# Norm sums on VectorE with a second ones-matmul, the input's first rows loaded ahead of the weights, and moved gates, low parts and scans in a two-layer hybrid block

## The chip, the cores and the metric

The kernel runs on one core of a Trainium2 chip. The metric is the time of one execution in device microseconds. Its engines are called here as in the profile: PE (TensorE: matmuls; PEld is its weight load), DVE (VectorE), ACT (ScalarE), POOL (GpSimd) and SP, whose queue issues nearly all DMA transfers. Each engine works through its own list of instructions in a fixed order, and an instruction that waits holds up all those behind it on that engine.

## The reference

Two layers work on a sequence of 1024 tokens with 1024 features. Layer 0 has a mixer of chunked retention and a gated delta rule (GDN), layer 1 a mixer with a gated linear recurrence (RG-LRU); each is followed by a feed-forward block with a short convolution. A root-mean-square norm over the features stands ahead of each of these four parts and at the end.

```python
def _rms(x):
    xf = x.astype(jnp.float32)
    return xf * lax.rsqrt(jnp.mean(xf * xf, axis=-1, keepdims=True) + EPS)

def retention_deltanet_mixer(hn, pos, w_in, conv_w, a_log, dt_bias, out_gain, w_out):
    q_r, k_r, v_r, g_r, q_d, k_d, v_d, g_d, b_d, a_d = jnp.split(hn @ w_in, split_at, axis=-1)
    ...
    beta = jax.nn.sigmoid(b_d.astype(f32))
    g = -jnp.exp(a_log.astype(f32)) * jax.nn.softplus(a_d.astype(f32) + dt_bias.astype(f32))
    y_d = gated_delta_chunkwise(q_d, k_d, v_d, g, beta)
    ...
def conv_ffn(hn, w_up, conv_w, conv_b, w_down):
    up = causal_dwconv(hn @ w_up, conv_w) + conv_b
    gate, val = jnp.split(up, 2, axis=-1)
    return (jax.nn.silu(gate) * val) @ w_down
```

Inside `gated_delta_chunkwise` each chunk of 64 tokens needs a triangular system solved before its values and state can be worked out.

## The kernel before

**Matmuls in three parts.** Features lie on the 128 partitions, tokens along the free axis. A product of two float32 matrices is formed from three matmuls in a reduced float32 format (`fp32r`), 128x128 times 128x512: high by high, low by high, and high by low (L296, L297, L298). 9000 of them make up nearly all of PE's work. The weights come in quarters of 256 KB: SP loads one into a `raw` buffer (L248), ACT rounds it to `whi` (L258), and `wlo`, the rest, is formed by a subtraction (L259), on POOL in the first mixer and on DVE after it (`lo_engine`). In the last part, the down-projection of the second feed-forward block, the tokens are worked in pieces of 512, 256 and 256, and each piece loads and splits its 16 quarters again.

**Order.** The program is written with generators: `project_n` emits matmuls, and after each group it lets "lanes" advance by one step. A lane holds the GDN work (key convolutions, gates, the per-chunk stages, the solution of the triangular system `subst`, its `merge`, the scans). A wait in a lane, `yield from range(k)`, puts off what follows by k groups. The framework then places the instructions on each engine's list by its own estimates; after that all order is fixed.

**The start.** SP loads `cols` (513 columns of per-feature constants, 256 KB), then three weight quarters, then the input `xT` in 16 pieces (8 feature blocks k for each half n of the tokens), with three more weight quarters ahead of k=4. ACT and DVE turn each piece into a high part (L371) and a low part (L372), and 24 matmuls on zeros (L1389) run while nothing else can.

**A norm.** For each k ACT squares the piece (L380 for k=0, into the accumulator; L389 for the others, into one of two buffers), and L391 adds the square to the accumulator. The add is on POOL, or on DVE past a block number called `on_vector`; where there are two accumulators, L394 adds them. Four matmuls with a column of ones (L404 in `norm_tok`) sum over the partitions, DVE (L408) and POOL (L409) form the power -1/2, and L416 in `norm_row` spreads the result over the partitions, in PSUM. There are eight norms of 512 tokens ahead of the four parts, and three in the last part (512, 256 and 256 tokens).

**The operands after a mixer.** `pair_operands` forms the first feed-forward operands from the mixer's output: it copies the spread row from PSUM to SBUF (L543, ACT), multiplies by it (L534, L551), and splits into high (L547, ACT) and low parts (L548, DVE).

**The GDN gates.** `gates()` makes 32 matmuls into two PSUM tiles, evacuates them on DVE (L1054), and transposes the result (L1058). In the program it stands behind the three key convolutions' `conv_tail` (L1098, L1101 on DVE, of 1024 columns each). After `subst`, whose steps are chains of small DVE operations (L1164, L1166), the solution is written to DRAM (L1169, L1171) and read back in another layout (L1185) for `merge` (L1198 on PE).

Of the kernel before, what the change touches and what calls it, by code (L numbers as in the profile page):

```python
# [13 lines left out]
F32 = mybir.dt.float32  # L14
F32R = mybir.dt.float32r
AF = mybir.ActivationFunctionType
ALU = mybir.AluOpType
# [86 lines left out]
class Block:  # L104
    def __init__(self, ctx, tc, I, out, stop=None):
        self.ctx, self.tc, self.nc, self.I, self.out = ctx, tc, tc.nc, I, out
        nc = tc.nc
        pool = lambda n, b, **k: ctx.enter_context(tc.tile_pool(name=n, bufs=b, **k))
        self.perm = pool("perm", 1)
        self.wraw_p = pool("wraw", 7)  # L110
        self.kept = pool("kept", 4)
        self.parts = pool("parts", 1)
        self.wsp = pool("wsp", RING)
        self.tp = pool("tp", 3)
        self.sm = pool("sm", 2)
# [61 lines left out]
    def quarter_order(self):  # L177
# [8 lines left out]
        for layer in range(2):  # L186
# [11 lines left out]
            o += [x for _ in range(2 + layer) for x in out(f"ffn_d{layer}", 1)]  # L198
# [56 lines left out]
    def split_quarter(self, raw, eng, w=HALF):  # L255
# [4 lines left out]
        return hi, lo  # L260

# [103 lines left out]
    def norm_step(self, st, k, gain, n):  # L365
# [7 lines left out]
        self.square_step(st, k, src)  # L373

    def square_step(self, st, k, src, w=HALF, on_vector=KT):

        nc = self.nc
        if k in (0, on_vector):
            acc = (st["bufs"][0 if k == 0 else 3] if "bufs" in st else self.t())[:, 0:w]
            nc.scalar.activation(acc, src, AF.Square)  # L380
            st.setdefault("acc", []).append(acc)
            return
# [7 lines left out]
        eng = nc.vector if k > on_vector else nc.gpsimd  # L390
        eng.tensor_tensor(st["acc"][-1], st["acc"][-1], sq, ALU.add)  # L391
        if on_vector < k == KT - 2:
            a, b = st["acc"]
            nc.vector.tensor_tensor(b, a, b, ALU.add)  # L394
            st["acc"] = [b]
# [48 lines left out]
    def part(self, ys, name, groups, sl, each):  # L444
# [27 lines left out]
    def down_x(self, ys, name, gain):  # L472

        def then(n, st, m, h):
            self.norm_step(st, m, gain, n)
# [4 lines left out]
    def down_pairs(self, ys, name, gain):  # L480
# [3 lines left out]
        def then(n, st, m, h):  # L484
            st["bufs"] = [self.halo[n][:, 4 + HALF:]] + [b[:, 4:4 + HALF] for b in self.halo] + \
                [self.R[:, n * HALF:(n + 1) * HALF]]
            self.square_step(st, m, h, on_vector=5)
# [34 lines left out]
    def pair_operands(self, st, n, gain, gap):  # L522
# [19 lines left out]
        row = (self.R[:, 0:HALF], self.halo[1][:, 4 + HALF:4 + T])[n]  # L542
        A.copy(row, st["row"])  # L543
# [255 lines left out]
    def final(self, ys, name):  # L799
# [13 lines left out]
        def part(t0, w, left):  # L813
# [4 lines left out]
            def each(m, h):  # L818
                self.square_step(st, m, h, w, on_vector=4 if t0 > 0 else KT)
                for f in left.get(m, ()):  # L820
                    f()
            self.part(ys, name, self.groups(1), sl, each)
            return st, sl

        run = self.run
# [17 lines left out]
    def rglru(self, gain):  # L843
        nc, I = self.nc, self.I
        V, A = nc.vector, nc.scalar

        sm = lambda name: self.perm.tile([P, 8], F32, name=name)
# [12 lines left out]
        xr, st = {}, {}  # L860
        stack = ExitStack()
        pool = stack.enter_context(self.tc.tile_pool(name="lru", bufs=1))
# [112 lines left out]
    def mix0(self, gain):  # L975
# [8 lines left out]
        self.og = self.perm.tile([P, 1], F32, name="og")  # L984
        self.nc.vector.tensor_scalar(self.og, self.col("out_gain", 0), 0.5, None, ALU.mult)
# [16 lines left out]
    def _mix0(self, room):  # L1002
# [385 lines left out]
        for _ in range(24):  # L1388
# [17 lines left out]
        for n in range(2):  # L1406
            sl = slice(n * HALF, (n + 1) * HALF)
            st = {}
# [11 lines left out]
        for h in range(3):  # L1420
            conv_tail("k", h, bufs[h], H[h])
        gdn += [gates()]
        self.step(self.lanes["gdn"])
        for h in range(3):
            gdn += [a_stage(h, i) for i in range(2)]
        conv_head("k", 3, K[3])
        gdn += [a_stage(3, i) for i in range(2)]

        def subst():
# [7 lines left out]
            yield from range(8)  # L1437
# [29 lines left out]
        self.lo_engine = V  # L1467
        gdn = self.lane("gdn", 2, 0)
        gdn += [scan(n) for n in range(NCH)]
# [14 lines left out]
    def _mix0_out(self, gain, gd):  # L1484
        nc, I = self.nc, self.I
        V = nc.vector

# [106 lines left out]
```

## Time and profile before

| | |
|---|---|
| median of 3 runs | 2300.38 us (2290.4 to 2300.4) |
| the profiled execution | 2299.97 us |
| its span, first to last instruction | 2298.2 us |
| mean granted TensorE clock | 0.985 |
| busy: DVE, ACT, POOL | 1714.5, 1094.5, 209.0 us |
| DMA | 307.45 MB, 133 GB/s over the span |

The profile gives busy times by engine, the span in 40 slices, and groups of instructions by source line with their number, mean duration and the idle time ahead of them. "Waits" lists the time that an engine stood still by the instruction that then came and the one that released it. "Windows" gives the same busy times for chosen stretches, with the granted clock of PE. The "timeline" has single instructions with their start and duration. A line of the profile names a source line of the kernel before; the changed kernel's lines stand up to about 20 further on.

### The profile page before, as it was taken

The page shows a single profiled execution, that of the slowest core. Times are in us where ns is not written, and L with a number is a line of the kernel's source. Part 1 is how long each engine was busy: PE and PEld are TensorE (multiplying, and loading weights), DVE is VectorE, ACT ScalarE, POOL GpSimd, SP SyncE. Part 2 cuts the span into 40 slices and gives each one's busy share as a digit, 9 for nine tenths or more (in the row PEclk, how much of TensorE's full clock was granted, in tenths as well). Part 3 has the DMA queues.
Part 4 walks back from the last instruction along what each step waited for, and adds up shares of the span by engine and source line. Part 5 has one row for each costly group of instructions (what it writes and reads, how often), then busy time and mean ns, then how long its engine had stood idle before and what let it go on. Part 6 is the DMA issues. An engine that isn't in the chain of part 4 may idle for free.

```text
span 2298.2 us, 30084 instructions
## 1 busy us (share of the span) xinstructions
PE 2248.9 (98%) x10784; PEld 1823.5 (79%) x10784; DVE 1714.5 (75%) x2532; ACT 1094.5 (48%) x1748; POOL 209.0 (9%) x160
## 2 busy tenths in 40 slices
PE   8999999999999999999999999999999999999997
PEld 7777788887888888888778888888788888877787
DVE  6886666556888888887874577768888888878747
ACT  5332433224655555554432466665555555553333
POOL 5331111220200000000000200002000000000003
PEclk9998999999999999999999999999999999999999
DMA  4242422414224544536465311142245444375554
GB/s 152 71 126 80 125 77 84 133 60 158 85 82 157 173 157 154 176 111 221 162 199 180 93 55 65 62 152 74 69 161 179 152 169 170 110 240 169 165 186 156
DMA packets 201110, 307.45 MB, mean 134 GB/s; under 512 B 31584, under 2 KB 89088, under 8 KB 200960
## 3 DMA queue, kind: packets, MB, share of 16 engines
q1 hardware_dynamic: 200528, 303.95, 40.2%
q8 instruction: 85, 1.39, 0.3%
q10 hardware_dynamic: 432, 1.58, 0.2%
q14 instruction: 65, 0.53, 0.1%
HBM read 214.73 MB, written 90.72 MB: 133 GB/s over the span
## 4 chain that ended last, share of the span: by engine, by line
PE 85%; DMA 6%; DVE 6%; issue 1%; ACT 1%; SPq 0%; POOL 0%; POOLq 0%; DVEq 0%; ACTq 0%
PE ps L296 26%; PE ps L298 26%; PE ps L297 26%; DMA s<-pf_dram 1%; DMA raw<-in_ffn_w_dram 1%; DVE t L1098 1%; DMA t<-yf_dram 1%; DVE l L1164 1%; DMA h<-in_xT_dram 1%; DMA t<-sf_dram 0%; DVE s L548 0%; PE pc L416 0%; DVE l L1166 0%; PE pc L1305 0%; PE pc L298 0%
## 5 line engine op out<-in xcount | busy, mean ns | idle before, releaser
L296 PE MATMUL ps<-s,whi 128*128 128x512 f32 (+1 forms) x3000 | 1188.5, 397 | 11.3 <-ACT whi L258 4.2
L297 PE MATMUL ps<-s,whi 128*128 128x512 f32 (+1 forms) x3000 | 1167.2, 389 | 10.7 <-DVE s L548 5.2
L298 PE MATMUL ps<-s,wlo 128*128 128x512 f32 (+1 forms) x3000 | 1164.6, 389 | 1.4 <-DVE wlo L259 1.4
L258 ACT CAST whi<-raw 128x512 fp32r<-128x512 f32 (+1 forms) x662 | 398.0, 605 | 740.0 <-PE ps L297 652.2
L296 PEld LDWEIGHTS ps<-s,whi 128*128 128x128 f32 x3000 | 568.3, 189 | 138.4 <-ACT whi L258 8.5
L297 PEld LDWEIGHTS ps<-s,whi 128*128 128x128 f32 x3000 | 569.2, 190 | 135.8 <-DVE s L548 6.7
L298 PEld LDWEIGHTS ps<-s,wlo 128*128 128x128 f32 x3000 | 568.1, 189 | 132.8 <-DVE wlo L259 2.1
L259 DVE TENSOR_TENSOR wlo<-raw,whi 128x512 fp32r<-128x512 f32 x632 | 428.7, 683 | 96.1 <-ACT whi L258 90.5
L670 DVE SCALAR_TENSOR_TENSOR t<-halo,cols,t 128x1024 f32<-128x1024 f32 x176 | 221.6, 1281 | 2.4 <-ACT t L668 1.2
L643 DVE TENSOR_TENSOR halo<-ps,kept 128x512 f32<-128x512 f32 (+1 forms) x138 | 92.0, 668 | 108.0 <-PE ps L298 107.7
L391 POOL TENSOR_TENSOR t<-t 128x512 f32<-128x512 f32 (+1 forms) x41 | 54.0, 1317 | 1295.2 <-ACT t L389 684.3
L653 DVE TENSOR_TENSOR h<-ps,h 128x512 f32<-128x512 f32 x112 | 77.0, 689 | 79.0 <-PE ps L298 78.8
L668 ACT ACTIVATE t<-halo,cols 128x1024 f32<-128x1024 f32 x88 | 109.4, 1246 | 15.7 <-DVE halo L643 9.0
L638 ACT COPY kept<-ps 128x512 f32<-128x512 f32 (+1 forms) x138 | 77.0, 558 | 1.4 <-PE ps L298 1.4
L461 DVE TENSOR_TENSOR h<-ps,h 128x512 f32<-128x512 f32 (+1 forms) x72 | 45.2, 627 | 28.9 <-PE ps L298 28.9
L259 POOL TENSOR_TENSOR wlo<-raw,whi 128x512 fp32r<-128x512 f32 x30 | 44.7, 1496 | 140.0 <-ACT whi L258 109.0
L755 DVE TENSOR_TENSOR t<-t 128x1024 f32<-128x1024 f32 x44 | 53.7, 1220 | 0.0
L738 ACT CAST s<-t 128x512 fp32r<-128x512 f32 x64 | 39.6, 622 | 26.3 <-DMA t<-sf_dram 17.2
L361 DVE TENSOR_TENSOR halo<-ps,R 128x512 f32<-128x512 f32 x38 | 25.9, 686 | 34.6 <-PE ps L298 32.9
L750 ACT ACTIVATE t<-t 128x1024 f32<-128x1024 f32 x44 | 46.8, 1063 | 8.0 <-DVE t L670 8.0
L1098 DVE SCALAR_TENSOR_TENSOR t<-halo,cols,t 128x1024 f32<-128x1024 f32 x33 | 46.4, 1414 | 3.8 <-ACT t L1096 3.4
L739 DVE TENSOR_TENSOR s<-t,s 128x512 fp32r<-128x512 f32 x64 | 42.6, 689 | 7.4 <-ACT s L738 7.0
(270 smaller groups left out, 1837.7 us busy)
## 6 DMA issues: line engine op xcount, KB each, us to landing
raw<-in_ffn_up_dram SPq DMA_DIRECT2D x176, 256.0 KB, 2.8
s<-pf_dram SPq DMA_DIRECT2D x96, 256.0 KB, 5.6
yf_dram<-t SPq DMA_DIRECT2D x32, 512.0 KB, 2.9
sf_dram<-t SPq DMA_DIRECT2D x64, 256.0 KB, 3.0
t<-sf_dram SPq DMA_DIRECT2D x64, 256.0 KB, 4.0
raw<-in_ffn_w_dram SPq DMA_DIRECT2D x64, 256.0 KB, 3.2
raw<-in_mix_in_dram SPq DMA_DIRECT2D x62, 256.0 KB, 3.0
pf_dram<-t SPq DMA_DIRECT2D x48, 256.0 KB, 3.0
```

Source lines behind the costliest of these rows:

```text
L258: self.nc.scalar.copy(hi[:, 0:w], raw[:, 0:w])
L259: eng.tensor_tensor(lo[:, 0:w], raw[:, 0:w], f32(hi[:, 0:w]), ALU.subtract)
L296: mm(ps, whi, xhi, start=start, stop=False)
L297: mm(ps, whi, xlo, start=False, stop=False)
L298: mm(ps, wlo, xhi, start=False, stop=stop)
L391: eng.tensor_tensor(st["acc"][-1], st["acc"][-1], sq, ALU.add)
L638: A.copy(kept[o], ps)
L643: V.tensor_tensor(dst(i, j), v(ps), v(kept[k]), ALU.add)
L653: V.tensor_tensor(h(*to[o]), ps.rearrange("p (h c) -> p h c", c=256), h(*to[o]), ALU.add)
L668: A.activation(t, buf[:, 2:2 + T], AF.Identity, scale=w(0), bias=self.col(f"ffn_cb{layer}", tile_i))
L670: V.scalar_tensor_tensor(t, buf[:, 2 + j:2 + j + T], w(j), t, ALU.mult, ALU.add)
L1098: V.scalar_tensor_tensor(c, buf[:, 1 + j:1 + j + T], w(j), c, ALU.mult, ALU.add)
```

## The change

It has eight parts.

1. The first 40 columns of `cols` (the gains) are loaded alone, the other 473 after the first half of the input. Each input piece is loaded ahead of the weights, the zero matmuls go from 24 to 14, and a piece's square is formed after the next piece's high and low part.
2. All squares are added on DVE. The last one (k=7) is not added: `norm_tok` takes it as a second accumulator, so that it makes eight matmuls where it made four (four where it made two for 256 tokens). L391's POOL adds and L394 are gone.
3. `pair_operands` reads the spread row from PSUM; the copy L543 is gone.
4. The first mixer's low parts of the weights are formed on DVE.
5. `gates()` stands ahead of the three key convolutions' tails, the last keys' `a_stage` comes two steps later, `subst` ends with two more empty steps, and the scans start six steps later.
6. In the last part the 16 weight quarters are loaded and split once and kept for all three pieces.
7. `rglru`'s small constants move into that layer's own pool, and `og` into `_mix0_out`; both were formed at the program's start before.
8. Nothing in the code of the retention's queries and gates is altered.

```diff
-        nc.sync.dma_start(self.cols, I["cols"])
+        self.ngain = COLS["gdn_conv"][0]
+        nc.sync.dma_start(self.cols[:, 0:self.ngain], I["cols"][:, 0:self.ngain])
...
-        self.lo_engine = nc.gpsimd
+        self.lo_engine = nc.vector
...
-            o += [x for _ in range(2 + layer) for x in out(f"ffn_d{layer}", 1)]
+            if layer == 0:
+                o += [x for _ in range(2) for x in out("ffn_d0", 1)]
...
+    def load_kept(self, src, i):
+        w = src.shape[1]
+        raw = self.raw()[:, 0:w]
+        self.nc.sync.dma_start(raw, src)
+        place = [self.slots1(j)[:, 0:w] for j in (i, i + 1)]
+        self.split_half(raw, place)
+        return place
...
         nc.scalar.activation(sq, src, AF.Square)
-        eng = nc.vector if k > on_vector else nc.gpsimd
-        eng.tensor_tensor(st["acc"][-1], st["acc"][-1], sq, ALU.add)
-        if on_vector < k == KT - 2:
-            a, b = st["acc"]
-            nc.vector.tensor_tensor(b, a, b, ALU.add)
-            st["acc"] = [b]
+        if k == KT - 1:
+            st["acc"].append(sq)
+        else:
+            nc.vector.tensor_tensor(st["acc"][0], st["acc"][0], sq, ALU.add)
...
-                    hi, lo = self.quarter((name + "ab"[u], m))
+                    if kept is None:
+                        hi, lo = self.quarter((name + "ab"[u], m))
+                    else:
+                        if (u, m) not in kept:
+                            kept[u, m] = self.load_kept(self.I[name + "ab"[u]][m], 4 * m + 2 * u)
+                        hi, lo = kept[u, m]
...
-        row = (self.R[:, 0:HALF], self.halo[1][:, 4 + HALF:4 + T])[n]
-        A.copy(row, st["row"])
+        row = st["row"]
...
-        for _ in range(24):
+        for _ in range(14):
             PE.matmul(ps[:, 0:P], warm[:, 0:P], warm[:, 0:P], start=True, stop=True)
...
             for k in range(KT):
-                if n == 0 and k in (0, 4):
-                    load_w(k // 4)
                 nc.sync.dma_start(H[k][:, sl], I["xT"][k * P:(k + 1) * P, sl])
-                self.norm_step(st, k, "g_mix0", n)
+                src[k] = self.norm_step(st, k, "g_mix0", n)
+                if n == 0 and k in (0, 3):
+                    load_w(k // 3)
+                if k:
+                    self.square_step(st, k - 1, src[k - 1])
+            self.square_step(st, KT - 1, src[KT - 1])
             if n == 0:
+                nc.sync.dma_start(self.cols[:, self.ngain:], I["cols"][:, self.ngain:])
...
-        for h in range(3):
-            conv_tail("k", h, bufs[h], H[h])
         gdn += [gates()]
         self.step(self.lanes["gdn"])
         for h in range(3):
+            conv_tail("k", h, bufs[h], H[h])
+        for h in range(3):
             gdn += [a_stage(h, i) for i in range(2)]
         conv_head("k", 3, K[3])
-        gdn += [a_stage(3, i) for i in range(2)]
+        gdn += [iter(range(2))] + [a_stage(3, i) for i in range(2)]
...
             subst_store(*sub)
-            yield from range(8)
+            yield from range(10)
...
-        gdn += [scan(n) for n in range(NCH)]
+        gdn += [iter(range(6))] + [scan(n) for n in range(NCH)]
```

What this does to the lists of the engines is shown at three places. The first is the head of ACT's list in the kernel before. `s_94` is a high part of the input, `h_86` and `h_87` its first pieces, `whi` a weight's high part, and DMAHW names a transfer that a row waits for.

```order
L1069 ACT_TABLE_LOAD
L1069 ACTIVATE l_114<-cols 128x4 [waits DMAHW0_49]
L1403 CAST whi<-raw 128x512 [waits DMAHW1_49]
L1403 CAST whi<-raw 128x512 [waits DMAHW2_49]
L1403 CAST whi<-R 128x512 [waits DMAHW3_49]
L960 ACTIVATE sple<-sple 128x8 [waits DVE_49]
L371 ACTIVATE s_94<-h_86,cols 128x512 [waits DMAHW4_49]
L380 ACTIVATE t<-h_86 128x512
L371 ACTIVATE s_94<-h_87,cols 128x512 [waits DMAHW5_49]
```

The same place in the changed kernel, where L383 is the old L371, L1417 the old L1403 and L392 the old L380:

```order
L383 ACT_TABLE_LOAD [waits DMAHW1_49]
L383 ACTIVATE s_94<-h_86,cols 128x512 [waits DMAHW0_49]
L1417 CAST whi<-raw 128x512 [waits DMAHW2_49]
L1417 CAST whi<-raw 128x512 [waits DMAHW3_49]
L1417 CAST whi<-R 128x512 [waits DMAHW4_49]
L383 ACTIVATE s_94<-h_87,cols 128x512 [waits DMAHW5_49]
L392 ACTIVATE t<-h_86 128x512
```

The first input piece now stands ahead of the weights, and the table load, which waited for nothing, waits for that piece's transfer.

The second place is DVE's list around the evacuation of the gates' two PSUM tiles (`t<-ps,R` 32x512) in the kernel before. The rows of 128x1024 are the tails of the key convolutions.

```order
L1101 SCALAR_TENSOR_TENSOR h_86<-h_86,t 128x1024 [waits Activation_49]
L1098 SCALAR_TENSOR_TENSOR t<-halo_97,cols,t 128x1024 [waits DVE_49]
L1098 SCALAR_TENSOR_TENSOR t<-l_114,cols,t 128x1024 [waits DVE_49]
L1101 SCALAR_TENSOR_TENSOR h_87<-h_87,t 128x1024 [waits Activation_49]
L1098 SCALAR_TENSOR_TENSOR t<-l_114,cols,t 128x1024 [waits DVE_49]
L1054 TENSOR_TENSOR t<-ps,R 32x512 [waits PE_49] x2
L1101 SCALAR_TENSOR_TENSOR h_88<-h_88,t 128x1024 [waits Activation_49]
```

In the changed kernel L1068 is the old L1054, L1112 the old L1098:

```order
L1068 TENSOR_TENSOR t<-ps,R 32x512 [waits PE_49]
L1112 SCALAR_TENSOR_TENSOR t<-halo_96,cols,t 128x1024 [waits Activation_49,Pool_49]
L1112 SCALAR_TENSOR_TENSOR t<-halo_97,cols,t 128x1024 [waits Activation_49,Pool_49]
L1112 SCALAR_TENSOR_TENSOR t<-halo_96,cols,t 128x1024 [waits DVE_49]
L1068 TENSOR_TENSOR t<-ps,R 32x512 [waits PE_49]
L1112 SCALAR_TENSOR_TENSOR t<-halo_96,cols,t 128x1024 [waits DVE_49]
```

Both evacuations stand at the head of the tails, with three tail rows between them, instead of behind all but one of the tail rows. On PE's list the first transposes still come after the gates' 32 matmuls, now 12 projection matmuls behind them, before 34.

The third place is the end of `subst` on DVE's list before. The rows on `l_114` are the solution, the copy L1170 its last step, and the rows `<-ps,R` evacuate projections.

```order
L1166 TENSOR_TENSOR l_114<-l_114 128x2x30 [waits DVE_49]
L1164 TENSOR_TENSOR l_114<-l_114 128x31 [waits DVE_49]
L1166 TENSOR_TENSOR l_114<-l_114 128x31 [waits DVE_49]
L1170 COPY l_114<-l_114 128x1024 [waits DVE_49]
L361 TENSOR_TENSOR t<-ps,R 128x512 [waits PE_49]
L999 SCALAR_TENSOR_TENSOR t<-t 128x1024 [waits Activation_49]
```

In the changed kernel L1180 is the old L1166, L1178 the old L1164, L1184 the old L1170:

```order
L1180 TENSOR_TENSOR l_112<-l_112 128x2x30 [waits DVE_49]
L262 TENSOR_TENSOR wlo<-raw,whi 128x512 [waits DMAHW2_49,PE_49,Activation_49]
L1178 TENSOR_TENSOR l_112<-l_112 128x31 [waits DVE_49]
L1180 TENSOR_TENSOR l_112<-l_112 128x31 [waits DVE_49]
L1184 COPY l_112<-l_112 128x1024 [waits DVE_49]
L373 TENSOR_TENSOR halo_96<-ps,R 128x512 [waits PE_49]
L262 TENSOR_TENSOR wlo<-raw,whi 128x512 [waits DMAHW4_49,Activation_49]
```

Low parts of weights (`wlo`) now stand between the steps. The evacuation behind the copy is that of the projection group that ends with PE's 600th projection matmul; before it was that of the 576th or so. The first `merge` matmul stands on PE's list behind 660 projection matmuls, before behind 614.

More of the change, by code (lines that the diff above doesn't have):

```diff
@@ L441, in steps, with part @@
         self.after(slots, go)
-    def part(self, ys, name, groups, sl, each):
+    def part(self, ys, name, groups, sl, each, kept=None):
         w = sl.stop - sl.start
@@ L474, in then @@
         def then(n, st, m, h):
-            self.norm_step(st, m, gain, n)
+            self.square_step(st, m, self.norm_step(st, m, gain, n))
             if m == KT - 1:
@@ L484, in then @@
         def then(n, st, m, h):
-            st["bufs"] = [self.halo[n][:, 4 + HALF:]] + [b[:, 4:4 + HALF] for b in self.halo] + \
-                [self.R[:, n * HALF:(n + 1) * HALF]]
-            self.square_step(st, m, h, on_vector=5)
+            st["bufs"] = [self.halo[n][:, 4 + HALF:]] + [b[:, 4:4 + HALF] for b in self.halo]
+            self.square_step(st, m, h)
             if m == KT - 1:
@@ L818, in each @@
             def each(m, h):
-                self.square_step(st, m, h, w, on_vector=4 if t0 > 0 else KT)
+                self.square_step(st, m, h, w)
                 for f in left.get(m, ()):
                     f()
-            self.part(ys, name, self.groups(1), sl, each)
+            self.part(ys, name, self.groups(1), sl, each, kept)
             return st, sl
+        kept = {}
         run = self.run
@@ L845, in rglru @@
         V, A = nc.vector, nc.scalar
-        sm = lambda name: self.perm.tile([P, 8], F32, name=name)
+        xr, st = {}, {}
+        stack = ExitStack()
+        pool = stack.enter_context(self.tc.tile_pool(name="lru", bufs=1))
+        sm = lambda name: pool.tile([P, 8], F32, name=name)
         sp = sm("sp")
@@ L1486, in _mix0_out @@
         V = nc.vector
+        self.og = self.perm.tile([P, 1], F32, name="og")
+        V.tensor_scalar(self.og, self.col("out_gain", 0), 0.5, None, ALU.mult)
         order = (4, 5, 6, 0, 7, 1, 2, 3)
```

18 lines of the change are left out of this document (6 added, 12 removed).

## The prediction

> **What bounds the kernel.** I read the page first, then PE's waits, then windows around the longest of them.
>
> ```profile
> PE 2248.9 (98%) x10784; PEld 1823.5 (79%) x10784; DVE 1714.5 (75%) x2532; ACT 1094.5 (48%) x1748; POOL 209.0 (9%) x160
> PE 85%; DMA 6%; DVE 6%; issue 1%; ACT 1%; SPq 0%; POOL 0%; POOLq 0%; DVEq 0%; ACTq 0%
> ```
>
> PE is busy 98% and carries 85% of the chain that ended last. The number of large matmuls doesn't change, so time can be won only where PE stands still (2298.2 - 2248.9 = 49 us) or runs slowly. The waits on PE say whom it stood for (engine, tile and line that waited, the releaser; us in total, times, longest):
>
> ```profile
> PE ps L297 <- DVE s L548: 5.2, 6, 1.4
> PE ps L297 <- DVE s L372: 5.1, 2, 4.8
> PE pc L404 <- DVE t L391: 3.2, 1, 3.2
> PE pc L1285 <- DMA l<-v_dram: 3.1, 1, 3.1
> PE ps L296 <- ACT s L547: 3.1, 2, 1.5
> PE pc L1058 <- DVE t L1054: 3.0, 1, 3.0
> PE pc L1198 <- DMA l<-t_dram: 2.5, 1, 2.5
> PE ps L298 <- DVE wlo L259: 1.4, 1, 1.4
> ```
>
> They make 26.6 us, and the change touches each of these places. Behind such a wait the granted clock falls. The windows around them (length; then PE, PEld, DVE, ACT, POOL busy; clock; DMA share; GB/s):
>
> ```profile
> 21.00:32.00 11.00, 8.90 (x25) 7.35 (x26) 9.68 (x22) 5.19 (x9) 4.09 (x4) 0.53 0.30 107
> 74.00:80.00 6.00, 5.73 (x22) 4.41 (x23) 3.84 (x12) 1.80 (x4) 2.43 (x4) 0.72 0.13 44
> 80.00:120.00 40.00, 38.07 (x196) 30.88 (x195) 34.28 (x78) 14.73 (x29) 10.96 (x7) 1.00 0.28 78
> 200.00:226.00 26.00, 23.53 (x180) 15.85 (x180) 8.78 (x17) 8.96 (x18) 2.56 (x2) 0.61 0.20 44
> 284.00:292.00 8.00, 4.91 (x22) 4.05 (x21) 3.94 (x6) 0.00 (x0) 4.16 (x3) 0.79 0.32 95
> 640.00:666.00 26.00, 21.65 (x138) 19.48 (x137) 20.00 (x23) 12.78 (x23) 1.02 (x1) 0.80 0.07 21
> 1612.00:1636.00 24.00, 19.55 (x127) 17.58 (x127) 19.81 (x22) 12.87 (x21) 1.02 (x1) 0.86 0.08 23
> ```
>
> A clock of c over w us means that PE did (1-c)w less than it could: 5.2 us at 21, 1.7 at 74, 10.1 at 200, 1.7 at 284, 5.2 and 3.4 at the two places where `pair_operands` works. So waits and clock together are some 50 us that the change could reach.
>
> **The change part by part**, against the profiled execution (2299.97 us, 0.4 below the median).
>
> *The start.*
>
> ```profile
> 0.73 1.28 ACT L1069 ACT_TABLE_LOAD   x1 [0.73 <-PEq L1586]
> 3.53 0.21 ACT L1069 ACTIVATE l<-cols 128x4 f32<-128x4 f32 x1 [1.51 <-DMA cols<-in_cols_dram]
> 7.72 0.72 ACT L371 ACTIVATE s<-h,cols 128x512 fp32r<-128x512 f32 x1 [0.84 <-DMA h<-in_xT_dram]
> 8.50 0.51 PE L296 MATMUL ps<-s,whi 128*128 128x512 f32 x1
> 15.21 6.61 POOL L391 TENSOR_TENSOR t<-t 128x512 f32<-128x512 f32 x4 [0.43 <-ACT t L389]
> 20.19 0.63 ACT L380 ACTIVATE t<-h 128x512 f32<-128x512 f32 x1 [1.10 <-POOL t L391]
> 23.10 0.79 PE L297 MATMUL ps<-s,whi 128*128 128x512 f32 x1 [4.79 <-DVE s L372]
> ```
>
> The first input piece was the fifth transfer and reached ACT at 7.72. Now only 40 columns stand ahead of it. I take its landing at 3.5, where `cols` landed before (the ACT row at 3.53); the table load now waits for it and adds its 1.28, the high part 0.72 and 0.7 for the weight behind it: first matmul at 6.2, **2.3 us** earlier. The 14 zero matmuls cover most of that time. The stall at 18.3 is ACT waiting for POOL's adds at 1.65 us each (6.61/4), which hold the two square buffers; on DVE an add takes 0.69 (row below). The 4.8 us go; what is late next is the first norm's last square, for which I leave 1.0. Without the stall the clock stretch of 5.2 goes too; I take 4.5. The two norms here have 16 more ones-matmul records:
>
> ```profile
> 594.67 0.39 PE L298 MATMUL ps<-s,wlo 128*128 128x512 f32 x1
> 594.90 0.95 PE L404 MATMUL pc<-ones,R 128*128 128x1 f32 x8
> L391 DVE TENSOR_TENSOR R<-R,halo x8: 684/692/695, 587.5 to 1610.2; 128x512 f32<-128x512 f32 x8
> L543 ACT COPY R<-pc x2: 587/587/587, 599.7 to 1569.7; 128x512 f32<-128x512 f32 x2
> ```
>
> Eight records take 0.95 us, about 0.9 of it on PE's path: -1.8. Sum of the start: 2.3 + 4.8 - 1.0 + 4.5 - 1.8 = **+9** (0 if the transfers hold the start, 11 at best).
>
> *The gates.*
>
> ```profile
> 72.35 1.28 DVE L1098 SCALAR_TENSOR_TENSOR t<-l,cols,t 128x1024 f32<-128x1024 f32 x1
> 73.55 1.27 DVE L1054 TENSOR_TENSOR t<-ps,R 32x512 f32<-32x512 f32 x2
> 74.27 0.43 PE L1058 MATMUL pc<-ident,t 32*128 32x32 f32 x4 [2.99 <-DVE t L1054]
> ```
>
> The evacuations waited behind the tails. Now three tail rows of 1.28 stand between them, 3.8 us, while the second tile's 16 matmuls take 3.7 (16 x 0.23, from a large matmul's start at 594.67 to the next row's at 594.90), and the transposes come 12 matmuls, 2.8 us, later. The wait goes, and with it the clock stretch: 3.0 + 1.7 = **+4.7** (3 to 5).
>
> *Low parts on DVE, in the first mixer.*
>
> ```profile
> L259 POOL TENSOR_TENSOR wlo<-raw,whi 128x512 fp32r<-128x512 f32 x30 | 44.7, 1496 | 140.0 <-ACT whi L258 109.0
> L259 DVE TENSOR_TENSOR wlo<-raw,whi 128x512 fp32r<-128x512 f32 x632 | 428.7, 683 | 96.1 <-ACT whi L258 90.5
> L1098 DVE SCALAR_TENSOR_TENSOR t<-halo,cols,t 128x1024 f32<-128x1024 f32 x33 | 46.4, 1414 | 3.8 <-ACT t L1096 3.4
> ```
>
> DVE gets 30 x 0.683 = 20.5 us. It had 34.28 of 40 us busy from 80 to 120; five or six more low parts would make it 38. Against that, L1098 has a mean of 1414 where one with POOL idle takes 1280 ns: 33 x 0.134 = 4.4 us come back from this line alone. DVE stays just under full, so I take -3 (0 if hidden, -20.5 if none is).
>
> *`subst` and `merge`.*
>
> ```profile
> 195.69 1.13 DVE L1170 COPY l<-l 128x1024 f32<-128x1024 f32 x1
> 202.48 0.31 PE L1198 MATMUL pc<-l,h 32*32 32x32 f32 x2 [2.47 <-DMA l<-t_dram]
> ```
>
> From the copy to `merge` 6.8 us pass (write and read of DRAM). PE's list had 38 matmuls (8.8 us) between the projection group evacuated behind the copy and `merge`; now 60 (14.0), but of the 5.2 us between these some 2 are used up, since the steps of `subst` share DVE with low parts. I count 3 us more slack against 2.5 of wait: the wait goes and the clock stretch behind it, of which I take 8.5 of 10.1: **+11** (0 to 12).
>
> *Scans.*
>
> ```profile
> 278.30 0.43 SPq L1454 DMA_DIRECT2D v_dram<-t  x1
> 285.67 0.32 SPq L1269 DMA_DIRECT2D l<-v_dram  x1
> ```
>
> The first scan matmul, L1285, waits for the last v to be written to DRAM and read back, 7.4 us from one issue to the next and then the landing. This chain stays. But `merge` starts later, so that some 30 more of its records stand on PE's list between the v projections and L1285: 30 x 0.14 (26 us for 180 records at 200) = 4 us of cover against a wait of 3.1. The wait goes, and half of 1.7: **+4** (0 to 5).
>
> *`pair_operands`, twice.* Gone are the copy (0.59) and an add on DVE (0.69); eight more records are added (-0.9, twice per place): 2 x (2 x 1.3 - 1.8) = 1.6, and a little from squares that no longer queue behind POOL, say **+2**; the clock stretches of 5.2 and 3.4 I leave as they are (+7 if they go). *The two norms behind the first feed-forward block:* their chains of squares run beside matmuls, their added records don't: 2 x 0.9 = **-1.8**.
>
> *The last part.*
>
> ```profile
> 2284.76 0.28 PE L298 MATMUL ps<-s,wlo 128*128 128x256 f32 x1
> 2286.34 0.43 DVE L394 TENSOR_TENSOR t<-t 128x256 f32<-128x256 f32 x1
> ```
>
> The last matmul ends at 2285.0, the span 13.2 us later. The add of the two accumulators (L394) and that of the last square behind it leave this tail, 0.9 us, and the evacuation of the last piece, which came to DVE behind such adds, follows PE sooner; I take 13.2 to 10.5. The 1.4 us for a low part (L259 among the waits) go, since none is formed any more in the last two pieces. Costs: 0.9 + 0.45 records. +2.7 + 1.4 - 1.3 = **+3**. The constants moved to `rglru` are small operations beside 98% PE: 0.
>
> Sum: 9 + 4.7 - 3 + 11 + 4 + 2 - 1.8 + 3 = 29; 2300 - 29 = **2271 us**.
>
> **A rule against it.** The wait ahead of `merge` was 2.47 us, and the clock then stood at 0.61 for 26 us. The Trainium skill, "TensorE: Matmul & The Clock Gate" (section "HAM oscillation"), states that PE must not idle for more than about 3.4 us. By that rule the wait at 200 is too short to have cost the clock, something else slows PE there, and the time would be 2282 (the first rival below). The trace speaks against the figure: at 71 a wait of 2.99 us is followed by 0.72 as well, and before L1285 one of 3.1 by 0.79, both under 3.4.
>
> **The rivals.**
>
> *The clock stays low among merges* (0.22). Merges are many small matmuls (180 records in 26 us, against 196 in 40 at full clock), so they may themselves keep the clock low, and the wait may only shift. Then 11 are lost: 2282. For it: the clock stayed low for 20 us after a short wait. Against it: it was full while PE was fed at 80 to 120, with small matmuls among the large.
>
> *DVE becomes the bound of the first mixer* (0.14). If none of the 20.5 us hides, 17.5 more than I took are lost: 2288. For it: 34.28 of 40. Against it: POOL's tensor operations slow DVE, and go.
>
> *The transfers hold the start* (0.08). Seven weights and constants and 16 pieces come over the same queue in any order; if the second half of the input is late anyway, the start's 9 are lost: 2280.
>
> *Doubled ones-matmuls bring the clock down* (0.05): slower. Sixteen records of one column in a row take 1.8 us in which PE does almost nothing; with a short wait beside them they could start a stretch as at 21, 5.2 us. Eleven norms cost up to 57, and from the sixth on (29/5.2) the gain is gone; with eight, 2313. Against it: the block of eight at 594.90 is followed by full speed.
>
> *The change doesn't do all it says.* The moved retention gates show in no line of the diff; that part is worth 0 and is in no sum.
>
> **How the numbers follow.** The forecast has 0.51: 2260 to 2281, its lower end with one pair's clock gained, its upper with the scan and pair terms missing and DVE a little worse. The rivals have 0.49 together and lie from 2280 to 2288, but for the slower one at 2313. A range of 2257 to 2290 leaves out that one, and the upper half of the DVE case. What a measurement can tell from no change is about 0.5%, 11.5 us: faster means below 2289. The forecast, the first and third rival and somewhat over a third of the second lie there, less something for two of them coming together: 0.80. Same is 0.14. Slower is 0.06, the last rival and a hundredth for DVE holding up more than its own work.
>
> **What would show it.** PE's waits without L372 at 4.8, L1058, L1198 and L1285; a clock near 1.0 from 20 to 30 and through the merges; the first large matmul near 6.2; L404's successor with 160 records; no POOL low parts. Wrong: PE waiting for low parts or evacuations between 60 and 220 with DVE full (DVE case), a low clock among merges without a wait ahead (first rival), or new stretches of low clock behind the norms.

## The result, and the profile after

The changed kernel takes 2270.18 us (median of 4, 2267.84 to 2270.97), the kernel before 2297.33 (2290.4 to 2300.4): a ratio of 0.9884, 95% interval 0.9857 to 0.9911. With the comparisons below the kernel before ran 40 times, from 2287.7 to 2301.4 us. Its profiled execution, at 2299.97, was among its long ones; the changed kernel's, at 2267.84, is the fastest of its four, which lie within 3.1 us. So the two traces differ by more than the medians.

Here is the page's line of busy times for the changed kernel, and the rows that head PE's waits now:

```profile
PE 2240.0 (99%) x10844; PEld 1821.3 (80%) x10844; DVE 1702.1 (75%) x2576; ACT 1073.4 (47%) x1712; POOL 78.8 (3%) x73
PE ps L308 <- ACT whi L261: 4.7, 6, 1.3
PE ps L309 <- DVE s L562: 2.3, 2, 1.1
PE ps L308 <- ACT s L561: 2.1, 2, 1.0
PE pc L1389 <- DVE l L1394: 1.8, 2, 0.9
PE pc L414 <- ACT t L401: 0.9, 1, 0.9
```

PE idles for 26 us of its span of 2266.0, where it idled for 49. Of the waits quoted for the kernel before, those at the start (L372, now L384), the gates (L1058, now L1072), `merge` (L1198, now L1212), the first scan (L1285, now L1299) and the low part (L259) are gone. Those at the pairs (L547 and L548, now L561 and L562) are halved: 8.3 us to 4.4. The last norm's wait went from 3.2 to 0.9.

The windows of the changed kernel, with the same columns as before; its merges run from 193 to 250 us:

```profile
21.00:32.00 11.00, 10.82 (x57) 8.84 (x57) 9.74 (x19) 7.31 (x14) 1.51 (x1) 1.00 0.34 119
74.00:80.00 6.00, 6.00 (x27) 4.83 (x26) 5.16 (x15) 3.36 (x4) 0.00 (x0) 1.00 0.25 83
150.00:190.00 40.00, 40.00 (x175) 32.32 (x175) 36.59 (x79) 8.07 (x10) 0.00 (x0) 1.00 0.37 129
205.00:245.00 40.00, 40.00 (x475) 28.15 (x474) 26.07 (x47) 23.24 (x51) 0.00 (x0) 1.00 0.47 115
608.00:634.00 26.00, 22.97 (x161) 21.71 (x160) 20.51 (x23) 12.85 (x21) 1.01 (x1) 0.87 0.05 17
1580.00:1606.00 26.00, 22.89 (x163) 21.70 (x162) 19.77 (x22) 12.87 (x22) 1.01 (x1) 0.87 0.04 11
```

The clock is full everywhere in the first mixer, through 475 PE records in 40 us at the merges too. It still falls at both pair sites. DVE is at 36.59 of 40 us from 150 to 190, and PE doesn't wait there.

To see where the time went, the matmul records of the three lines L296 to L298 (L308 to L310 after; 9096 in each trace) are numbered by their start. The table gives the start of the n-th in both profiled executions:

| n | what lies before it | before | after | gained so far | by this stretch |
|---|---|---|---|---|---|
| 144 | the start | 55.48 | 46.65 | 8.8 | 8.8 |
| 264 | the gates | 96.66 | 83.07 | 13.6 | 4.8 |
| 614 | per-chunk stages, `subst` | 199.61 | 181.84 | 17.8 | 4.2 |
| 1700 | merges and scans | 584.66 | 550.78 | 33.9 | 16.1 |
| 2200 | first pair site | 695.31 | 660.43 | 34.9 | 1.0 |
| 5500 | layer 0's feed-forward with its norms, part of layer 1's mixer | 1475.40 | 1444.01 | 31.4 | -3.5 |
| 6260 | the rest of that mixer, second pair site | 1645.89 | 1614.47 | 31.4 | 0.0 |
| 8600 | second feed-forward | 2198.16 | 2168.80 | 29.4 | -2.0 |
| end | the last part | 2298.18 | 2266.01 | 32.2 | 2.8 |

### The profile page after: what moved, and what is told of

Same layout as the page of the kernel before. It is cut to its first block, busy times and chain, and to the rows that moved or that the text cites. A ratio compares the mean times of both kernels' runs of the same rounds, so it can differ in the third digit from the quotient of the medians.

```text
span 2266.0 us, 29902 instructions
## 1 busy us (share of the span) xinstructions
PE 2240.0 (99%) x10844; PEld 1821.3 (80%) x10844; DVE 1702.1 (75%) x2576; ACT 1073.4 (47%) x1712; POOL 78.8 (3%) x73
## 4 chain that ended last, share of the span: by engine, by line
PE 92%; DVE 3%; DMA 3%; issue 1%; ACT 1%; POOL 0%; SPq 0%; POOLq 0%; DVEq 0%; ACTq 0%
PE ps L308 28%; PE ps L309 28%; PE ps L310 28%; DMA t<-sf_dram 1%; PE pc L414 1%; DMA t<-y_dram 1%; PE pc L426 0%; PE pc L1319 0%; PE pc L309 0%; PE pc L310 0%; PE pc L308 0%; PE pc L1338 0%; PE pc L1361 0%; PE pc L1252 0%; DVE s L562 0%
## 5 line engine op out<-in xcount | busy, mean ns | idle before, releaser
L308 PE MATMUL ps<-s,whi 128*128 128x512 f32 (+1 forms) x2856 | 1132.4, 397 | 9.6 <-ACT whi L261 4.7
L309 PE MATMUL ps<-s,whi 128*128 128x512 f32 (+1 forms) x2856 | 1121.4, 393 | 3.9 <-DVE s L562 2.3
L310 PE MATMUL ps<-s,wlo 128*128 128x512 f32 (+1 forms) x2856 | 1118.4, 392 | 0.0
L261 ACT CAST whi<-raw 128x512 fp32r<-128x512 f32 x614 | 373.1, 612 | 713.3 <-PE ps L309 623.9
L308 PEld LDWEIGHTS ps<-s,whi 128*128 128x128 f32 x2856 | 538.9, 189 | 137.0 <-ACT whi L261 7.9
L309 PEld LDWEIGHTS ps<-s,whi 128*128 128x128 f32 x2856 | 540.0, 189 | 127.7 <-DVE s L753 5.7
L310 PEld LDWEIGHTS ps<-s,wlo 128*128 128x128 f32 x2856 | 538.7, 189 | 124.9 <-DVE wlo L262 0.9
L262 DVE TENSOR_TENSOR wlo<-raw,whi 128x512 fp32r<-128x512 f32 x614 | 410.3, 673 | 76.9 <-ACT whi L261 71.3
L684 DVE SCALAR_TENSOR_TENSOR t<-halo,cols,t 128x1024 f32<-128x1024 f32 x176 | 221.7, 1279 | 2.3 <-ACT t L682 1.1
L419 POOL TENSOR_TENSOR rtok<-rtok,npow 128x4 f32<-128x4 f32 (+1 forms) x11 | 11.4, 1032 | 1782.8 <-DVE rtok L418 1728.8
L401 ACT ACTIVATE t<-h 128x512 f32<-128x512 f32 (+1 forms) x49 | 27.2, 562 | 46.8 <-DVE h L477 40.8
L308 PE MATMUL ps<-s,s 128*128 128x256 f32 (+1 forms) x144 | 46.1, 320 | 0.0
L310 PE MATMUL ps<-s,s 128*128 128x256 f32 (+1 forms) x144 | 45.8, 318 | 0.0
```

What stands on the lines that cost most here:

```text
L261: self.nc.scalar.copy(hi[:, 0:w], raw[:, 0:w])
L262: eng.tensor_tensor(lo[:, 0:w], raw[:, 0:w], f32(hi[:, 0:w]), ALU.subtract)
L308: mm(ps, whi, xhi, start=start, stop=False)
L309: mm(ps, whi, xlo, start=False, stop=False)
L310: mm(ps, wlo, xhi, start=False, stop=stop)
L684: V.scalar_tensor_tensor(t, buf[:, 2 + j:2 + j + T], w(j), t, ALU.mult, ALU.add)
```

## The experiments

Ten kernels ran: changed kernels with one part undone, and kernels before with one part or one number changed. Times are medians; "against the changed kernel" is against 2270.18. The runs of different comparisons may be on different chips, so differences of a microsecond or two are left to the traces.

**The low parts back on POOL.**

```diff
-        self.lo_engine = nc.vector
+        self.lo_engine = nc.gpsimd
...
+        self.lo_engine = V
         gdn = self.lane("gdn", 2, 0)
         gdn += [iter(range(6))] + [scan(n) for n in range(NCH)]
```

> The changed kernel with the first mixer's low parts of the weights back on POOL, all else as changed. On PE's list this also moves the first merge matmul from behind 660 projection matmuls back to behind 621, though subst still ends with ten empty steps. Theory: the later merge came with the low parts, not with the empty steps; so the wait ahead of merge (about 2.5 us) and a clock near 0.6 for some 20 us come back, and waits on DVE among the per-chunk stages too: 2270 becomes 2279 to 2286. Rival: the low parts only load DVE, and merge is covered by the other edits: 3 us faster than the changed kernel, 2267, clock full from 180 to 210.

It took 2287.66 us (2283.52 to 2292.43), 17.5 above the changed kernel; 0.9972 of the kernel before, 0.9959 to 0.9985. That is above what the theory gave, and the rival has the wrong sign. Its PE waits between 60 and 240 us, and the window behind the start of merge:

```profile
PE pc L1088 <- DVE l L1085: 3.7, 1, 3.7
PE pc L1212 <- DMA l<-t_dram: 3.0, 1, 3.0
PE pc L1137 <- DVE h L1149: 1.5, 2, 0.8
198.00:222.00 24.00, 24.00 (x217) 16.45 (x216) 10.55 (x20) 10.40 (x21) 2.34 (x2) 0.64 0.20 41
```

Merge's wait and its low clock are back (0.64 over 24 us), though subst's two extra empty steps are still there. The gates, which are still early, meet a wait one step later in their chain, at L1088. DVE's rows from 48 to 200 us show one reason. The convolution tails and the first line of `subst`, of this kernel and then of the changed one (busy us, mean ns):

```profile
L1112 DVE SCALAR_TENSOR_TENSOR t<-halo,cols,t 128x1024 f32<-128x1024 f32 x21 | 29.8, 1428 | 0.1
L1178 DVE TENSOR_TENSOR l<-l 128x31 f32<-128x31 f32 (+15 forms) x31 | 14.5, 469 | 0.8
```

```profile
L1112 DVE SCALAR_TENSOR_TENSOR t<-halo,cols,t 128x1024 f32<-128x1024 f32 x24 | 30.4, 1276 | 0.7 <-ACT t L1110 0.6
L1178 DVE TENSOR_TENSOR l<-l 128x31 f32<-128x31 f32 (+15 forms) x31 | 10.5, 339 | 1.4 <-DMA l<-l_dram 0.8
```

The same DVE operations take 12% and 38% longer in the mean. A few rows make this difference, as the shortest, median and longest of the 31 rows of `subst` show (ns, the same two kernels):

```profile
L1178 DVE TENSOR_TENSOR l<-l x31: 192/375/1431, 150.3 to 187.8; 128x31 f32<-128x31 f32 x2, 128x60 f32<-128x60 f32 x2, 128x87 f32<-128x87 f32 x2, 128x112 f32<-128x112 f32 x2
L1178 DVE TENSOR_TENSOR l<-l x31: 183/358/426, 143.5 to 182.9; 128x31 f32<-128x31 f32 x2, 128x60 f32<-128x60 f32 x2, 128x87 f32<-128x87 f32 x2, 128x112 f32<-128x112 f32 x2
```

The other reason is the place on PE's list. The last DVE row that L1088 waits for, here and then in the changed kernel:

```profile
87.03 0.18 DVE L1085 TENSOR_TENSOR l<-l 128x32 f32<-128x32 f32 x1
89.73 0.18 DVE L1085 TENSOR_TENSOR l<-l 128x32 f32<-128x32 f32 x1
```

In the changed kernel it comes even later, and PE doesn't wait, because L1088 stands behind 293 projection matmuls there and behind 264 here. The first matmuls on the keys (L1137) moved likewise, from behind 293 to behind 270.

**The low parts on DVE, alone.**

```diff
-        self.lo_engine = nc.gpsimd
+        self.lo_engine = nc.vector
```

> The kernel before with one part of the change alone: the first mixer's low parts on DVE. Merge then stands behind 660 projection matmuls. Theory: merge's wait and clock stretch go (11 to 13 us) and the short waits on DVE between 110 and 160 us shrink since POOL no longer slows DVE (0 to 4): 2300 becomes 2284 to 2290. Rival: DVE becomes the bound of the first mixer and PE waits for low parts and evacuations: 2297 or more.

This one line of the change brought the kernel before from 2294.22 to 2278.07 us (0.9928, 0.9906 to 0.9949): 16.2 us, a little more than expected. PE's wait for the gates is gone, with their code where it was. The timeline of DVE at the convolution tails in the kernel before, and then in this one:

```profile
56.69 8.82 DVE L1098 SCALAR_TENSOR_TENSOR t<-halo,cols,t 128x1024 f32<-128x1024 f32 x5
73.55 1.27 DVE L1054 TENSOR_TENSOR t<-ps,R 32x512 f32<-32x512 f32 x2
```

```profile
56.62 7.26 DVE L1098 SCALAR_TENSOR_TENSOR t<-halo,cols,t 128x1024 f32<-128x1024 f32 x6
68.48 0.67 DVE L1054 TENSOR_TENSOR t<-ps,R 32x512 f32<-32x512 f32 x1
70.28 0.67 DVE L1054 TENSOR_TENSOR t<-ps,R 32x512 f32<-32x512 f32 x1
```

Five tails took 8.82 us beside POOL, 1.76 each, and six take 7.26, 1.21 each. So the second evacuation starts at 70.28, where both started at 73.55. DVE's busy time over the whole execution, 1714.5 us in the kernel before, didn't rise by the 20.5 us of the 30 added rows:

```profile
PE 2235.1 (98%) x10784; PEld 1813.7 (80%) x10784; DVE 1712.3 (75%) x2562; ACT 1095.0 (48%) x1748; POOL 163.8 (7%) x130
```

The line also changes PE's list: the framework, which places instructions by its own estimates, puts the first merge matmul behind 660 projection matmuls instead of 614.

**Only merge moved.**

```diff
             subst_store(*sub)
-            yield from range(8)
+            yield from range(24)
```

> The kernel before with one number changed: subst ends with 24 empty steps instead of 8, so that the first merge matmul stands behind 678 projection matmuls instead of 614. Theory: the wait of 2.5 us ahead of merge is what brings the clock down; both go: 2300 becomes 2287 to 2291, the clock is 0.95 or more where the merges now are. Rival: the many small matmuls of merge keep the clock low by themselves: only the wait goes, 2298, and the clock stays near 0.6 for 20 us behind the start of merge.

2281.90 us (2279.55 to 2284.52) against 2294.22: 0.9950, 0.9934 to 0.9966, 12.3 us, within the 9 to 13 of the theory. The window at its merges:

```profile
206.00:232.00 26.00, 26.00 (x229) 19.29 (x229) 17.10 (x23) 13.59 (x25) 5.67 (x4) 1.00 0.43 109
```

229 PE records in 26 us at full clock: the small matmuls alone don't bring the clock down.

**Merge moved a little.**

```diff
-            yield from range(8)
+            yield from range(14)
```

> The kernel before with 14 empty steps behind subst instead of 8: merge then stands behind 621 projection matmuls instead of 614, 1.6 us later. Theory: the wait of 2.5 us shrinks to about 0.9 us, which is too short to bring the clock down: nearly all of what 24 steps gave is there already, 2281 to 2286, clock 0.95 or more behind the start of merge. Rival: any wait ahead of the merges, among their small matmuls, is enough for the clock to fall: 2290 to 2293, clock near 0.6.

2290.27 us (ten runs, 2283.27 to 2293.62; 0.9982, 0.9967 to 0.9997). The median is the rival's. The only trace is that of the fastest of the ten executions, and it fits neither account; here are merge's wait, and the window around it:

```profile
PE pc L1198 <- DMA l<-t_dram: 3.0, 1, 3.0
200.00:224.00 24.00, 21.02 (x199) 14.11 (x197) 9.32 (x16) 11.29 (x22) 3.01 (x3) 0.93 0.30 65
```

The wait didn't shrink: seven matmuls more on PE's list were no cover. And 3.0 us of it left the clock at 0.93 here, where 2.5 and 3.0 us in the kernel before and with the low parts on POOL left 0.61 and 0.64. Windows cut to the stretch behind the wait show what differs, in the kernel before, with the low parts on POOL, and here:

```profile
202.46:222.94 20.48, 20.46 (x143) 13.66 (x143) 7.17 (x13) 6.31 (x13) 2.56 (x2) 0.50 0.19 45
198.44:215.51 17.07, 17.07 (x137) 11.56 (x137) 7.31 (x14) 7.00 (x14) 1.27 (x1) 0.50 0.15 24
204.35:207.76 3.41, 3.41 (x25) 1.84 (x23) 0.69 (x1) 2.67 (x5) 1.27 (x1) 0.50 0.22 33
```

Each time the clock falls to half at the wait's end or within 1.3 us of it. It stays there for 20.48, 17.07 and 3.41 us, and the length of the wait doesn't tell which. That the ten runs spread over 10 us, as do those of the kernel before, fits this: the longer executions have the lower mean clock (2283.27 us at 0.993 and 2293.62 at 0.987 here; 2287.72 at 0.993 and 2299.45 at 0.985 for the kernel before beside them). Only one execution of each has a trace.

**The low parts on POOL, with merge far behind.**

```diff
-        self.lo_engine = nc.vector
+        self.lo_engine = nc.gpsimd
...
-            yield from range(10)
+            yield from range(22)
```

> The changed kernel with the low parts on POOL and 22 empty steps behind subst, so that merge stands behind 678 projection matmuls while POOL still works beside DVE. Theory: of the 17 us that the low parts on POOL cost, merge's wait and clock come back as gain (9 to 11), and the wait of 3.7 us at the gates with its clock stretch, where POOL slows DVE, stays (6 to 8): 2276 to 2280. Rival: it is all DVE's slowness beside POOL, and merge's wait stays as long: 2285 to 2290.

2276.73 us (2273.43 to 2279.47; 0.9920, 0.9900 to 0.9940), as the theory had it. Of the 17.5 us that the low parts on POOL cost, 10.9 come back with merge's place alone; 6.5 stay (against the medians of two comparisons). In the traces a loss of 6.9 us stands at the 614th matmul already (188.78 against 181.84), with a wait of 2.9 us at L1088, which stands behind 264 matmuls here too, and nothing is lost behind the 614th.

**The gates back behind the tails.**

```diff
-        gdn += [gates()]
-        self.step(self.lanes["gdn"])
         for h in range(3):
             conv_tail("k", h, bufs[h], H[h])
+        gdn += [gates()]
+        self.step(self.lanes["gdn"])
```

> The changed kernel with the GDN gates back behind the three key convolutions' tails. Theory: PE waits for the gates' evacuation by about 3 us again and the clock falls for one stretch of 3.4 us: 2270 becomes 2274 to 2276. Rival: with POOL idle DVE is through the tails in time, and the order there is worth nothing: 2270, no wait of the transposes over 0.5 us.

2271.68 us, 1.5 above the changed kernel: nearer to the rival. No wait of the transposes comes back; DVE reaches the second evacuation in time:

```profile
61.06 0.67 DVE L1068 TENSOR_TENSOR t<-ps,R 32x512 f32<-32x512 f32 x1
61.66 1.26 DVE L1112 SCALAR_TENSOR_TENSOR t<-l,cols,t 128x1024 f32<-128x1024 f32 x1
62.85 0.67 DVE L1068 TENSOR_TENSOR t<-ps,R 32x512 f32<-32x512 f32 x1
```

What is left shows at another place: PE waits 1.4 us at L1252 near 136 us, which the changed kernel doesn't, and the clock is at 0.84 from 135 to 146. By the 614th matmul 2.9 us are lost (184.73 against 181.84), by the end 2.1.

**The adds of the squares on POOL.**

```diff
-            nc.vector.tensor_tensor(st["acc"][0], st["acc"][0], sq, ALU.add)
+            nc.gpsimd.tensor_tensor(st["acc"][0], st["acc"][0], sq, ALU.add)
```

> The changed kernel with the adds of the squares on POOL (the last square still a second accumulator). Theory: at the start POOL's adds hold the two square buffers again, so ACT and with it the second half of the input is late: a wait of some 5 us and a clock stretch of 5 us behind it come back; the pairs lose about 1 us each: 2270 becomes 2279 to 2285. Rival: the start was gained by the order of the transfers, and the adds hide: 2270 to 2273.

2278.80 us (0.9936, 0.9921 to 0.9951), 8.6 above the changed kernel. The profiled execution, at 2273.80, is at least 4.5 us faster than the other three, so its trace, 6.0 us longer than the changed kernel's, doesn't hold the whole difference. The timeline of its start:

```profile
14.69 8.27 POOL L405 TENSOR_TENSOR t<-t 128x512 f32<-128x512 f32 x5 [1.42 <-ACT t L401]
18.48 0.50 PE L309 MATMUL ps<-s,whi 128*128 128x512 f32 x1 [1.19 <-DVE s L384]
22.99 0.63 ACT L392 ACTIVATE t<-h 128x512 f32<-128x512 f32 x1 [2.04 <-POOL t L405]
21.00:32.00 11.00, 9.55 (x40) 7.99 (x39) 8.71 (x10) 7.61 (x13) 7.60 (x6) 0.69 0.39 131
```

ACT stands behind POOL's adds, PE behind the operands, and the clock falls to 0.69. The 54th matmul starts at 27.55, in the changed kernel at 19.81. By the 144th 7.2 us are lost, so the adds made most of the start's 8.8. The rest, 1.6, is what the order of transfers and zero matmuls gave: the first large matmul starts at 6.94, where it started at 8.50. At the pair sites the adds on POOL cost nothing that the trace shows (1.1 us ahead of them, regained behind).

**One accumulator, half the ones-matmuls.**

```diff
-        if k == KT - 1:
-            st["acc"].append(sq)
-        else:
+        if True:
             nc.vector.tensor_tensor(st["acc"][0], st["acc"][0], sq, ALU.add)
```

> The changed kernel with the last square added on DVE like the others, so that each norm has one accumulator and half the ones-matmuls. This takes 9 x 0.9 + 2 x 0.45 = 9 us of small matmuls from PE and puts an add of 0.7 us into each norm's chain. Theory: where the chain is hidden beside matmuls (seven norms or so) the doubled ones-matmuls were pure cost; where it is exposed (the pairs' second half twice, the start's first norm, the last piece) the two nearly cancel: 5 to 7 us faster than the changed kernel, 2263 to 2266. Rival: the added chain time comes back as waits with clock stretches behind them: 2270 to 2276.

2262.35 us (2261.93 to 2263.69; 0.9870 of the kernel before, 0.9855 to 0.9884). This is 7.8 less than the changed kernel, and none of its runs comes near that kernel's; by the spans of the profiled executions it is 5.8 (2260.2 against 2266.0). It is the fastest of all. The two kernels weren't in one comparison: against the kernel before of its own it gains 29.3 us, the changed kernel 27.2 against its own. The traces part by some 0.9 us at most norms of 512 tokens, hidden or not: 1.8 between the 4500th and the 5000th matmul, where layer 0's feed-forward has its two. It loses 1.4 between the 264th and the 614th, which isn't explained. Of the norms only the last piece's pays for the add, as the row of its wait shows (0.9 in the changed kernel):

```profile
PE pc L412 <- DVE t L403: 1.6, 1, 1.6
```

**The copy of the row.**

```diff
-        row = st["row"]
+        row = (self.R[:, 0:HALF], self.halo[1][:, 4 + HALF:4 + T])[n]
+        A.copy(row, st["row"])
```

> The changed kernel with the ACT copy of the spread row back in the operands after a mixer. Theory: 0.6 us in each of the two exposed chains, perhaps a longer clock stretch: 2271 to 2273. Rival: the chain's end isn't at the copy but at the casts behind it, which are paced by the matmul groups: 2270.

2273.09 us (2271.78 to 2275.89), 2.9 above. The waits for the pairs' low and high parts are nearly as long as in the kernel before (5.2 and 3.1), against 2.3 and 2.1 in the changed one:

```profile
PE ps L309 <- DVE s L563: 4.9, 5, 1.4
PE ps L308 <- ACT s L562: 3.3, 3, 1.5
```

In the traces it loses 1.8 us at the first site and 0.8 at the second, which is nearly all of the 2.9.

**The last part's weights loaded for each piece.** The quarters of the last product are put back into the order of loads, and `kept` is not used:

```diff
-            if layer == 0:
-                o += [x for _ in range(2) for x in out("ffn_d0", 1)]
+            o += [x for _ in range(2 + layer) for x in out(f"ffn_d{layer}", 1)]
...
-        kept = {}
+        kept = None
```

> The changed kernel with the last part's weights loaded and split anew for each piece, as before. Theory: the low parts come back between the last part's DVE rows: a wait of about 1.4 us for one of them and a later last evacuation, 2270 becomes 2272 to 2274. Rival: loads and splits hide beside the matmuls: 2270.

2271.69 us (2267.78 to 2272.70): 1.5 above, inconclusive, since its runs cover those of the changed kernel. From the 8600th matmul to the end its trace is 1.6 us longer than the changed kernel's.

## Why the prediction was right, and where its working was not

The forecast was 2271 us in a range of 2257 to 2290, and the time was 2270.18. Its base was the profiled execution of 2299.97; against that execution's trace the changed kernel's is 32.2 us shorter, where the sum gave 29. The median of the kernel before is lower than its profiled run, so the gain between medians is 27 in the first comparison, and about 24 against the median of 2294.22 in the largest one (16 runs).

- **The start, +9.** Measured 8.8. The adds on DVE gave 7.2, as argued: POOL held the square buffers. The order gave 1.6, less than 2.3, because the first input piece landed later than the 3.5 us assumed (rows of the changed kernel):

```profile
4.36 1.28 ACT L383 ACT_TABLE_LOAD   x1 [4.36 <-DMA h<-in_xT_dram]
5.66 0.72 ACT L383 ACTIVATE s<-h,cols 128x512 fp32r<-128x512 f32 x1
6.94 0.50 PE L308 MATMUL ps<-s,whi 128*128 128x512 f32 x1
```

  The table load did move behind that transfer. The 1.0 us left for the first norm wasn't needed. Some of the 8.8 is chance: b_subst24 and b_subst14, whose code for the start is that of the kernel before, reach the 144th matmul at 54.17 and 54.32 instead of 55.48, and against them the start gains 7.5 to 7.7. In their traces the clock is at half for 3.4 us there, in that of the kernel before for 10.2.
- **Low parts on DVE, -3.** This is the step that failed. It was priced as 20.5 us of work on a nearly full engine. The runs show it as the largest part of the change: 16.2 us alone, 17.5 when undone. Of the 17.5, 10.9 are merge's place, which the sum held under `merge`; 6.5 stand against the -3. DVE got the work and lost its neighbour: tails from 1.76 to 1.21 us, `subst`'s rows from 469 to 339 ns, and a busy time that fell from 1714.5 to 1712.3 us with the 30 rows added. The prediction credited only the tails, 4.4 us. How much of the 6.5 comes from DVE's faster rows, and how much from the later places of L1088 and L1137 on PE's list, no run parts.
- **The gates, +4.7.** The wait and its clock stretch went (4.8), but the move wasn't needed for it. With the low parts on DVE they go without the move (b_lo_dve), and with the move undone they stay away (a_gates_late, 1.5 us). With the move and POOL's low parts (a_lo_pool) the transposes don't wait either, but the next step of the chain does, 3.7 us.
- **`merge` +11 and scans +4.** Measured 16.1 together. That the wait, and not the merges, held the clock down is shown by b_subst24. The place behind 660 matmuls was read rightly from the order, but it came from the low parts, not from the empty steps: with ten of these and POOL's low parts merge's wait is there. The scan's cover was sized by 0.14 us a record, from a window at a clock of 0.61; at full clock 475 records take 40 us, 0.08 each, so 30 records cover 2.5 us and not 4. That wait goes in b_subst24 without the six empty steps. In b_lo_dve PE still waits 2.0 us at L1285, there put down to a low part on DVE; which edit removed the wait from the changed kernel isn't shown.
- **Per-chunk stages, 0.** They gained 4.2, which no term held; with the low parts on POOL the waits there are back (L1137, 1.5 us). With the low parts' -3 the sum was 7.2 too low here.
- **Pairs, +2.** Measured 1.0; the copy is worth some 1.8 and 0.8, less the doubled ones-matmuls. The clock stretches stayed, as forecast, the first of them shorter (0.80 over 26 us before, 0.87 after).
- **The doubled ones-matmuls** cost what was charged, 0.9 us per norm. What the prediction didn't ask is whether the part is worth having: without it the kernel is faster by 6 to 8 us.
- **The last part, +3.** Measured 2.8, of which some 1.6 came from the kept weights.
- **The rest:** -1.8 was charged for layer 0's two norms behind its feed-forward. The trace lost 3.5 and 2.0 us from there to the last part. Two traces of kernels that don't differ there part by up to 1.5 (between the 2320th and 4500th matmul, for a_lo_pool). But from the 6260th to the 8600th matmul all eight kernels with the change take 553.4 to 556.2 us and all four without it 551.5 to 552.3, so this is more than scatter, and its cause stays open.

That the total came so near is in part luck: the 7.2 us too little for the first mixer were offset by 3.7 us more lost behind the first pair site than was charged, and by 1.0 less at the pairs.

Of the rivals, the low clock among merges fell with b_subst24. DVE as the bound fell with b_lo_dve, which gained 16.2 us; in the changed kernel DVE was at 36.59 of 40 us and PE didn't wait there. The transfers as the bound of the start fell with a_pool_add, where the same order of transfers with POOL's adds lost 7.2 us. New clock stretches from doubled ones-matmuls don't show: the clock is full around the norms at the start, and the low windows left are those at the pair sites, which the kernel before had too.

As for the rule of the Trainium skill, "TensorE: Matmul & The Clock Gate" ("HAM oscillation"), that PE must not idle for more than about 3.4 us: with merge moved the low clock went with the wait, so a wait of 2.5 us did cost it, and the figure is no safe bound here.

## What to carry to other kernels

An engine that does a little elementwise work beside a busy one isn't free help: look at the mean of the same operation with and without the neighbour before leaving work there. Where a framework places instructions by its own estimates, moving one kind of work changes the order elsewhere; undo each part alone before crediting it. A short wait on PE can cost several times its length if the clock falls behind it, so a wait's worth is read with the granted clock of the window after it.

## What the runs showed of the hardware

- DVE's 128x1024 scalar_tensor_tensor goes at 1.21 us a row with POOL idle and at 1.76 in a run of five beside POOL's tensor_tensor. The small rows in `subst` have nearly the same median with POOL's work beside them (375 ns) and without (358), but the longest takes 1431 ns instead of 426.
- How long the clock stays down behind a wait isn't fixed by the wait's length: waits of 2.5, 3.0 and 3.0 us were followed by half clock for 20.48, 17.07 and 3.41 us, among the same matmuls.
- At the start with POOL's adds, two waits of 1.2 and 1.5 us were followed by half clock for 6.83 us, from 23.86 to 30.69 (0.69 over the window of 11 us).
